# A two-block transformer kernel: the modulation's accumulation and the activations' low part, both written on VectorE

## The chip, the cores and the metric

The kernel runs on one NeuronCore of a Trainium2 chip. The metric is the device time of one execution in microseconds (us). A NeuronCore has TensorE (PE in the profile, with its weight loads shown apart as PEld), VectorE (DVE), ScalarE (ACT), GpSimd (POOL) and SyncE (SP, which issues nearly all DMAs here). Each engine works through its own queue in the order in which the program wrote it, and waits at an instruction whose inputs are not there yet.

## The reference

Two transformer blocks work on 256 tokens of width 1024, all in fp32. The first has a SwiGLU feed-forward network, two attentions with a gated merge, and a second feed-forward network. The second has two layers, one with a sliding-window attention and one with a stick-breaking attention, each with a feed-forward network behind it. Six modulation vectors for each of these two layers come from a conditioning vector `c`:

```python
cond = jax.nn.silu(c)
for i in range(DEPTH_2):
    mod = (cond @ ada_w[i] + ada_b[i])[:, None, :]
    sh1, sc1, g1, sh2, sc2, g2 = jnp.split(mod, 6, axis=-1)
    ...
    h = rmsnorm_2(x, norm2_g[i]) * (1.0 + sc2) + sh2
    x = x + g2 * swiglu_2(h, w_gate[i], w_up[i], w_down[i])
...
swiglu_2 = (jax.nn.silu(h @ w_gate) * (h @ w_up)) @ w_down
```

`ada_w` is 2 x 1024 x 6144 fp32 values, 50 MB. The hidden width of every feed-forward network is 2816, which is 22 tiles of 128.

## The kernel before

Activations are kept transposed: channels on the 128 partitions, the 256 tokens along the free axis. TensorE takes fp32r operands, so each fp32 factor is cut into a high part (rounded) and a low part (the value minus its high part), and a product of two tiles is three matmuls, high by high, high by low and low by high (`mm3`, lines 270 to 273).

Weights come as 194 blocks of 16 tiles (1 MB each) through `Stream`. SyncE loads a block into one of four `raw` buffers. Each quarter block (128 x 512) is then cast on ScalarE (`wh`, line 211) and subtracted on VectorE (`wl`, line 219). `W.step`, called from `pump` after every four tile products, writes the next quarter into the queues, two blocks ahead of the block that TensorE works on; `wh` and `wl` have three buffers.

A feed-forward network (`ffn`) is 22 units of gate and up products, 48 matmuls each, and then 8 outputs of the down product, which take 11 weight blocks. I call these the gate-up part and the down part of FFN1 to FFN4. The activation of a unit is a generator, `epilogue`, of which `follow` takes one step after every fourth tile product of later units. Its steps before were: `tg` and `tu` on VectorE from PSUM (lines 493, 494; with a shift also two one-column copies `bb`, 497 and 498); `sg` on ScalarE (500); `a` on VectorE (505, or 503 with a shift); then, in one step, the high part `ah` on ScalarE (507) and the low part `al` on GpSimd (508). The PSUM tiles of one unit are used again two units later, so `tg` and `tu` free what TensorE needs next.

The modulation runs beside the feed-forward networks (`Ada`). It is a product of one row with a matrix, made without TensorE: a step takes one 128 x 1024 tile of `ada_w`, scales it by one column of `cs` and adds it to `acc`; eight steps give one modulation vector for each partition's share, and `reduce` sums over partitions by four pairs of VectorE transposes and reductions (452, 453) and four small matmuls (460). `A.tick` is called at the last quarter of each weight block, behind that block's third and before its last `wl`, and makes as many steps as the plan is behind: 24 steps beside FFN1, 32 each beside FFN2 and FFN3, 8 beside FFN4. Tiles are loaded up to three steps ahead into three buffers (423, 424). The step before:

```python
if kc == 0:
    self.acc = self.pool.tile([128, 1024], F32, tag="acc", bufs=2, name=nm("acc"))
    nc.scalar.activation(self.acc, raw, AF.Copy, scale=self.cs[:, 0:1])
else:
    nc.scalar.activation(raw, raw, AF.Copy, scale=self.cs[:, kc:kc + 1])
    nc.gpsimd.tensor_add(self.acc, self.acc, raw)
```

Of the kernel before, what the change touches and what calls it, by code (L numbers as in the profile page):

```python
# [10 lines left out]
F32 = mybir.dt.float32  # L11
F32R = mybir.dt.float32r
I32 = mybir.dt.int32
AF = mybir.ActivationFunctionType
ALU = mybir.AluOpType
# [3 lines left out]
S = 256  # L19
# [138 lines left out]
def hybrid_two_block_kernel(ctx: ExitStack, tc: tile.TileContext, x, w, ada, vecs, rows, pos, consts,  # L158
                            masks, out):
    nc = tc.nc  # L160
# [9 lines left out]
    def nm(s):  # L170
        count[0] += 1
        return f"{s}_{count[0]}"

    def mm_ps(shape):
        return pp.tile(shape, F32, tag="mm", bufs=4, name=nm("mm"))
# [5 lines left out]
    class Stream:  # L181
# [51 lines left out]
        def next(self, *names):  # L233
            i = self.taken
            assert {n for n, _, _ in plan[i]} <= set(names), (i, plan[i][0], names)
            self.prep(self.CUT * (i + 1))
            while any(d[0] == i for d in self.due):
                self.rest(len(self.due) - 1)
            self.taken += 1
            self.quarter = -1  # L240
            self.step()
            return self.hl.pop(i)

        def step(self):

            self.quarter += 1
            if self.quarter < 4:
                at = self.CUT * (self.taken - 1 + self.ahead) + self.quarter + 1
                self.prep(min(at, self.parts + 2))
            if self.quarter == 3:  # L250
                A.tick()
# [6 lines left out]
    def pump():  # L258
        for g in list(hooks):
            try:  # L260
                next(g)
            except StopIteration:
                hooks.remove(g)
        W.step()
# [5 lines left out]
    def mm3(ps, lh, ll, rh, rl, start, stop):  # L270
        nc.tensor.matmul(ps, lhsT=lh, rhs=rh, start=start, stop=False)  # L271
        nc.tensor.matmul(ps, lhsT=lh, rhs=rl, start=False, stop=False)  # L272
        nc.tensor.matmul(ps, lhsT=ll, rhs=rh, start=False, stop=stop)  # L273
# [111 lines left out]
    class Ada:  # L385
# [42 lines left out]
        def step(self):  # L428
            i = self.i
            if i >= self.last:  # L430
                return
            self.load(i + 3)
            cg, kc = divmod(i, DC)
            raw = self.raw.pop(i)
            if kc == 0:
                self.acc = self.pool.tile([128, 1024], F32, tag="acc", bufs=2, name=nm("acc"))
                nc.scalar.activation(self.acc, raw, AF.Copy, scale=self.cs[:, 0:1])
            else:
                nc.scalar.activation(raw, raw, AF.Copy, scale=self.cs[:, kc:kc + 1])  # L439
                nc.gpsimd.tensor_add(self.acc, self.acc, raw)  # L440
            self.i += 1
            if kc == DC - 1:
                l, g = divmod(cg, 6)
                self.due = (self.ticks + 2, self.reduce(self.acc, l, g))
# [36 lines left out]
    def ffn(pool, names, norm, shift, add_scale, after, pair=False, table=None):  # L481
        gate, up, down = names
        n = S + 2 if shift else S
        ah = pool.tile([128, FC, S], F32R, name=nm("ah"))
        al = pool.tile([128, FC, S], F32R, name=nm("al"))
        early, tails = [], []

        def epilogue(c, ps):
            tg = pool.tile([128, S], F32, tag="tg", bufs=2, name=nm("tg"))
            tu = pool.tile([128, S], F32, tag="tu", bufs=2, name=nm("tu"))  # L490
            sg = pool.tile([128, S], F32, tag="sg", bufs=2, name=nm("sg"))
            a = pool.tile([128, S], F32, tag="a", bufs=2, name=nm("a"))
            nc.vector.tensor_mul(tg, ps[0][:, :S], norm.r)  # L493
            nc.vector.tensor_mul(tu, ps[1][:, :S], norm.r)  # L494
            if shift:
                bb = pool.tile([128, 2], F32, tag="bb", bufs=2, name=nm("bb"))
                nc.vector.tensor_copy(bb[:, 0:1], ps[0][:, S:S + 1])
                nc.vector.tensor_copy(bb[:, 1:2], ps[1][:, S:S + 1])  # L498
            yield
            nc.scalar.activation(sg, tg, AF.Silu, bias=bb[:, 0:1] if shift else 0.0)  # L500
            yield
            if shift:
                nc.vector.scalar_tensor_tensor(a, tu, bb[:, 1:2], sg, op0=ALU.add, op1=ALU.mult)
            else:
                nc.vector.tensor_mul(a, tu, sg)  # L505
            yield
            nc.scalar.copy(ah[:, c], a)  # L507
            nc.gpsimd.tensor_sub(al[:, c], a, ah[:, c])  # L508

        def follow():  # L510
            tails.extend(epilogue(*e) for e in early)
            early.clear()
            for g in list(tails):
                if next(g, tails) is tails:
                    tails.remove(g)

        c = 0
        while c < FC:
            paired = c == 0 and pair
            bank = at_ps if c in (0, 3) else mm_ps  # L520
            units = [(c, W.next(gate, up), [bank([128, n]), bank([128, n])])]
            if paired:
                W.ahead = 1
                units.append((1, W.next(gate, up), [mm_ps([128, n]), mm_ps([128, n])]))
            order = [(u, half, kc) for u in units for half in range(2) for kc in range(DC)]
            if c == 0:
                order.sort(key=lambda o: o[2] + 3 * o[0][0])
            for i, ((_, (wh, wl), ps), half, kc) in enumerate(order):
                t = half * DC + kc
                mm3(ps[half], wh[:, t], wl[:, t], xgh[:, kc, :n], xgl[:, kc, :n], kc == 0, kc == DC - 1)  # L530
                if i % 4 == 3:
                    pump()
                if i % 4 == 1 and (c > 2 or c == 2 and (pair or i > 8)):
                    follow()
            W.ahead = 2
            early.extend((at, ps) for at, _, ps in units)
            c += len(units)
        while early or tails:
            follow()
        if table:  # L540
            nc.scalar.preload_act_table_set(table)
        i = 0
        for d in range(DC):
            p = mm_ps([128, S])
            for kc in range(FC):
                if i % 16 == 0:
                    wh, wl = W.next(down)
                mm3(p, wh[:, i % 16], wl[:, i % 16], ah[:, kc], al[:, kc], kc == 0, kc == FC - 1)
                i += 1
                if i % 4 == 0:  # L550
                    pump()
            s = add_scale if isinstance(add_scale, float) else add_scale[:, d:d + 1]
            nc.vector.scalar_tensor_tensor(xT[:, d], p, s, xT[:, d], op0=ALU.mult, op1=ALU.add)  # L553
            after(d)
# [269 lines left out]
    with ExitStack() as mix:  # L824
# [73 lines left out]
        with tc.tile_pool(name="merge", bufs=1) as gp:  # L898
# [5 lines left out]
            for d in range(DC):  # L904
                if d % 4 == 0:
                    bh, bl = W.next("w_up_b")
                if d == 0:
                    W.ahead = 1
                    ah, al = W.next("w_up_a")
# [203 lines left out]
    with ExitStack() as mix:  # L1113
# [12 lines left out]
        def after(steps, act):  # L1126
            for _ in range(steps):
                yield
            act()
# [67 lines left out]
        name = "wqkv_b_2"  # L1197
# [69 lines left out]
```

## Time and profile before

| | us |
|---|---|
| median of 3 runs (lowest, highest) | 1222.14 (1218.98, 1222.35) |
| the profiled execution | 1221.54 |
| its span, first to last instruction | 1219.7 |
| TensorE busy | 1178.0 (97%) |
| VectorE busy | 977.0 (80%) |
| ScalarE busy | 716.4 (59%) |
| GpSimd busy | 435.9 (36%) |

The profiled execution has 1.84 us around its span and lies 0.60 us below the median. The page's chain of work that ended last runs almost wholly through TensorE's matmuls of lines 271 to 273. Busy times are unions of an engine's instructions; the "mean ns" of a group is the mean length of one instruction, and two instructions that follow each other closely overlap a little in these records, so busy time is below count times mean. The idle column of a group is the idle time of the engine just before it and what ended that.

### The profile page before, as it was taken

Reading aid. Unit: us, or ns where it says so; the run is one execution under the profiler, and the core shown is the slowest. Engines: PE = TensorE matmul, PEld = TensorE weight load, DVE = VectorE, ACT = ScalarE, POOL = GpSimd, SP = SyncE. Lnnn points to the kernel's source line nnn. Section 1 sums busy time; section 2 is a strip of 40 time slices with the busy share of each in tenths; the row PEclk is TensorE's granted clock in tenths of the full one; section 3 lists DMA queues with packets and bytes.
Section 4 is the critical chain, followed back from the end, with each engine's and each line's share of the span. In section 5 each row is a group of like instructions: output and inputs, shape, how many; then the busy total and the mean of one; then the engine's idle time right before and its main releaser. Section 6 shows DMA issues by size and latency. Waiting matters only on the chain. (4 is left out here: it accounts for less than half of the span.)

```text
span 1219.7 us, 24926 instructions
## 1 busy us (share of the span) xinstructions
PE 1178.0 (97%) x9762; PEld 1138.4 (93%) x9762; DVE 977.0 (80%) x1886; ACT 716.4 (59%) x1420; POOL 435.9 (36%) x338
## 2 busy tenths in 40 slices
PE   8999999999999999988998999989899999999998
PEld 7999999999899998988997899989898889999998
DVE  8879997565668899999878789998987786777652
ACT  5666664455465666575466777656546666665441
POOL 4556442011303275665246046655510002342100
PEclk9999999999999999999998999999999999999999
DMA  8876666434344686865451277676663334764450
GB/s 315 291 299 247 240 240 234 174 140 172 110 158 148 244 294 217 322 260 217 173 180 70 82 255 286 246 289 246 230 243 135 117 134 173 263 248 163 166 196 37
DMA packets 45332, 251.74 MB, mean 206 GB/s; under 512 B 5280, under 2 KB 8096, under 8 KB 21536
## 3 DMA queue, kind: packets, MB, share of 16 engines
q1 hardware_dynamic: 44784, 248.78, 56.2%
q8 instruction: 77, 1.26, 0.4%
q10 hardware_dynamic: 432, 1.38, 0.3%
q14 instruction: 39, 0.32, 0.1%
HBM read 249.09 MB, written 1.05 MB: 205 GB/s over the span
## 5 line engine op out<-in xcount | busy, mean ns | idle before, releaser
L219 DVE TENSOR_TENSOR wl<-raw,wh 128x512 fp32r<-128x512 f32 x744 | 624.3, 877 | 60.6 <-ACT wh L211 59.2
L271 PE MATMUL mm<-xgh,wh 128*128 128x256 f32 (+1 forms) x1840 | 526.0, 286 | 12.4 <-DVE tg L493 7.1
L273 PE MATMUL mm<-xgh,wl 128*128 128x256 f32 (+1 forms) x1840 | 520.1, 283 | 0.0
L272 PE MATMUL mm<-xgl,wh 128*128 128x256 f32 (+1 forms) x1840 | 519.0, 282 | 0.0
L211 ACT CAST wh<-raw 128x512 fp32r<-128x512 f32 (+1 forms) x752 | 419.9, 613 | 162.0 <-PE mm L272 80.4
L271 PEld LDWEIGHTS mm<-xgh,wh 128*128 128x128 f32 x1840 | 348.0, 189 | 20.9 <-issue 20.5
L272 PEld LDWEIGHTS mm<-xgl,wh 128*128 128x128 f32 x1840 | 349.2, 190 | 0.0
L273 PEld LDWEIGHTS mm<-xgh,wl 128*128 128x128 f32 x1840 | 348.1, 189 | 0.3 <-DVE wl L219 0.3
L440 POOL TENSOR_TENSOR acc<-acc,ada 128x1024 f32<-128x1024 f32 x84 | 215.1, 2561 | 186.3 <-ACT ada L439 185.6
L273 PE MATMUL mm<-ah,wl 128*128 128x256 f32 x704 | 197.8, 281 | 3.1 <-DVE wl L219 3.1
L271 PE MATMUL mm<-ah,wh 128*128 128x256 f32 x704 | 197.8, 281 | 2.5 <-DVE bb L498 2.5
L272 PE MATMUL mm<-al,wh 128*128 128x256 f32 x704 | 197.3, 280 | 0.0
L273 PEld LDWEIGHTS mm<-ah,wl 128*128 128x128 f32 x704 | 132.7, 188 | 4.0 <-DVE wl L219 3.9
L271 PEld LDWEIGHTS mm<-ah,wh 128*128 128x128 f32 x704 | 132.9, 189 | 2.8 <-issue 2.6
L272 PEld LDWEIGHTS mm<-al,wh 128*128 128x128 f32 x704 | 133.1, 189 | 0.0
L340 POOL TENSOR_TENSOR ssq<-ssq,sq 128x256 f32<-128x256 f32 x49 | 41.9, 861 | 251.9 <-ACT sq L335 250.9
L508 POOL TENSOR_TENSOR al<-a,ah 128x256 fp32r<-128x256 f32 x88 | 94.7, 1079 | 98.8 <-ACT ah L507 98.8
L439 ACT ACTIVATE ada<-ada,cs 128x1024 f32<-128x1024 f32 x84 | 95.5, 1147 | 0.0
L335 ACT ACTIVATE sq<-xT 128x256 f32<-128x256 f32 x49 | 19.7, 412 | 83.6 <-DVE xT L553 75.1
L494 DVE TENSOR_TENSOR tu<-mm,rB 128x256 f32<-128x256 f32 x80 | 33.1, 414 | 44.2 <-PE mm L273 44.2
L860 POOL TENSOR_SCALAR bias<-M 128x384 f32<-128x384 f32 x20 | 25.5, 1281 | 100.7 <-DVE lo L702 100.1
L507 ACT CAST ah<-a 128x256 fp32r<-128x256 f32 x88 | 34.8, 398 | 44.0 <-DVE a L505 29.8
(201 smaller groups left out, 1465.0 us busy)
## 6 DMA issues: line engine op xcount, KB each, us to landing
raw<-in_w SPq DMA_DIRECT2D x185, 1024.0 KB, 5.4
ada<-in_ada SPq DMA_DIRECT2D x96, 512.0 KB, 3.9
raw<-in_w SPq DMA_DIRECT2D x8, 128.0 KB, 3.9
raw<-in_w SPq DMA_DIRECT2D x4, 256.0 KB, 5.1
out<-xT SPq DMA_DIRECT2D x8, 128.0 KB, 2.1
xT<-in_x SPq DMA_DIRECT2D x3, 256.0 KB, 4.5
M<-in_masks ACTq DMA_DIRECT2D x1, 768.0 KB, 4.3
Mstick<-in_masks ACTq DMA_DIRECT2D x1, 386.0 KB, 3.3
```

The costliest lines, as they stand in the source:

```text
L211: nc.scalar.copy(h[:, part], self.raw[i][:, part])
L219: engine.tensor_sub(l[:, part], self.raw[i][:, part], h[:, part])
L271: nc.tensor.matmul(ps, lhsT=lh, rhs=rh, start=start, stop=False)
L272: nc.tensor.matmul(ps, lhsT=lh, rhs=rl, start=False, stop=False)
L273: nc.tensor.matmul(ps, lhsT=ll, rhs=rh, start=False, stop=stop)
L340: nc.gpsimd.tensor_add(self.ssq, self.ssq, t)
L439: nc.scalar.activation(raw, raw, AF.Copy, scale=self.cs[:, kc:kc + 1])
L440: nc.gpsimd.tensor_add(self.acc, self.acc, raw)
L494: nc.vector.tensor_mul(tu, ps[1][:, :S], norm.r)
L507: nc.scalar.copy(ah[:, c], a)
L508: nc.gpsimd.tensor_sub(al[:, c], a, ah[:, c])
L860: nc.gpsimd.tensor_scalar(b, M[:, at:at + 384], slope, None, op0=ALU.mult)
```

## The change

The step of the modulation leaves ScalarE and GpSimd: its first product becomes one VectorE tensor-scalar operation, and each later scaling and addition becomes one VectorE operation, `acc = raw * cs + acc`. The low part `al` moves from GpSimd to VectorE and is written one step of `follow` later than `ah`, and `a` has three buffers instead of two. The title of the change also speaks of heads in pairs; the attention code is the same in both kernels.

```diff
             if kc == 0:
                 self.acc = self.pool.tile([128, 1024], F32, tag="acc", bufs=2, name=nm("acc"))
-                nc.scalar.activation(self.acc, raw, AF.Copy, scale=self.cs[:, 0:1])
+                nc.vector.tensor_scalar(self.acc, raw, self.cs[:, 0:1], None, op0=ALU.mult)
             else:
-                nc.scalar.activation(raw, raw, AF.Copy, scale=self.cs[:, kc:kc + 1])
-                nc.gpsimd.tensor_add(self.acc, self.acc, raw)
+                nc.vector.scalar_tensor_tensor(self.acc, raw, self.cs[:, kc:kc + 1], self.acc,
+                                               op0=ALU.mult, op1=ALU.add)
...
-            a = pool.tile([128, S], F32, tag="a", bufs=2, name=nm("a"))
+            a = pool.tile([128, S], F32, tag="a", bufs=3, name=nm("a"))
...
             yield
             nc.scalar.copy(ah[:, c], a)
-            nc.gpsimd.tensor_sub(al[:, c], a, ah[:, c])
+            yield
+            nc.vector.tensor_sub(al[:, c], a, ah[:, c])
```

On VectorE, one unit of the gate-up part of FFN2 was written like this before (`raw` and `wh` are a weight block and its high part, `mm` the PSUM tiles, `rB` the norm's factor):

```order
L493 TENSOR_TENSOR tg_5881<-mm_5797,rB_4841 128x256
L494 TENSOR_TENSOR tu_5882<-mm_5798,rB_4841 128x256
L219 TENSOR_TENSOR wl_5868<-raw_5719,wh_5867 128x512 x2
L505 TENSOR_TENSOR a_5884<-tu_5882,sg_5883 128x256
L219 TENSOR_TENSOR wl_5868<-raw_5719,wh_5867 128x512 x2
```

and a unit with two modulation steps is now:

```order
L493 TENSOR_TENSOR tg_6095<-mm_6002,rB_4820 128x256
L494 TENSOR_TENSOR tu_6096<-mm_6003,rB_4820 128x256
L219 TENSOR_TENSOR wl_6081<-raw_5921,wh_6080 128x512 x2
L505 TENSOR_TENSOR a_6098<-tu_6096,sg_6097 128x256
L219 TENSOR_TENSOR wl_6081<-raw_5921,wh_6080 128x512
L439 SCALAR_TENSOR_TENSOR acc_5899<-ada_5976,cs,acc_5899 128x1024
L439 SCALAR_TENSOR_TENSOR acc_5899<-ada_6064,cs,acc_5899 128x1024
L462 TENSOR_TENSOR modT_124<-at_6158,V 128x8
L219 TENSOR_TENSOR wl_6081<-raw_5921,wh_6080 128x512
L509 TENSOR_TENSOR al_5144<-a_6098,ah_5143 128x256
```

The two accumulations stand between the third and the fourth `wl` of the unit, and `al` stands last, ahead of the next unit's `tg`.

On GpSimd, the same part of FFN2 was written like this before:

```order
L440 TENSOR_TENSOR acc_5463<-acc_5463,ada_5541 128x1024
L440 TENSOR_TENSOR acc_5463<-acc_5463,ada_5617 128x1024
L508 TENSOR_TENSOR al_5165<-a_5652,ah_5164 128x256
L440 TENSOR_TENSOR acc_5463<-acc_5463,ada_5693 128x1024
L508 TENSOR_TENSOR al_5165<-a_5732,ah_5164 128x256
```

All of these are gone from GpSimd's queue, which goes from 325 rows to 153; VectorE's goes from 1573 to 1814 and ScalarE's loses the 96 modulation rows.

## Rows read from the trace of the kernel before

**Rows 1.** The page: each engine's busy time, share of the span, instructions

```profile
PE 1178.0 (97%) x9762; PEld 1138.4 (93%) x9762; DVE 977.0 (80%) x1886; ACT 716.4 (59%) x1420; POOL 435.9 (36%) x338
```

**Rows 2.** Stretches: FFN2 and FFN3 (gate-up, down), FFN1 and FFN4 (gate-up)

```profile
core 0: us, PE busy (x) PEld busy (x) DVE busy (x) ACT busy (x) POOL busy (x), PEclk, DMA share, GB/s
409.00:541.00 132.00, 123.27 (x1027) 122.03 (x1027) 126.57 (x175) 85.41 (x152) 77.42 (x43) 0.99 0.72 264
541.00:609.00 68.00, 62.26 (x531) 60.91 (x531) 59.72 (x93) 37.03 (x69) 29.58 (x21) 1.00 0.58 212
705.00:838.00 133.00, 125.14 (x1046) 123.99 (x1045) 125.71 (x213) 87.24 (x153) 76.88 (x43) 1.00 0.71 264
838.00:904.00 66.00, 62.29 (x534) 61.92 (x533) 61.66 (x92) 37.71 (x65) 27.60 (x16) 0.97 0.62 224
20.00:142.00 122.00, 121.14 (x1024) 120.88 (x1024) 105.07 (x169) 80.57 (x148) 64.44 (x39) 1.00 0.77 289
1031.00:1151.00 120.00, 119.86 (x1004) 119.49 (x1003) 88.70 (x205) 72.35 (x139) 39.03 (x31) 1.00 0.63 223
```

**Rows 3.** Waits of PE, 409 to 609, then 705 to 904: total us, times, longest

```profile
PE mm L271 <- DVE tg L493: 7.1, 5, 2.3
...
PE mm L271 <- DVE bb L498: 7.7, 5, 2.5
PE at L460 <- DVE adas L453: 3.7, 1, 3.7
```

**Rows 4.** Timelines of DVE, POOL and PE in FFN3's gate-up: start, us, instructions

```profile
791.40 4.02 DVE L219 TENSOR_TENSOR wl<-raw,wh 128x512 fp32r<-128x512 f32 x2
795.35 0.41 DVE L493 TENSOR_TENSOR tg<-mm,rB 128x256 f32<-128x256 f32 x1
...
791.16 2.59 POOL L440 TENSOR_TENSOR acc<-acc,ada 128x1024 f32<-128x1024 f32 x1
793.71 1.17 POOL L508 TENSOR_TENSOR al<-a,ah 128x256 fp32r<-128x256 f32 x1
...
796.30 0.36 PE L271 MATMUL mm<-xgh,wh 128*128 128x258 f32 x1 [2.41 <-DVE bb L498]
```

**Rows 5.** DVE groups: FFN4 down (wl), FFN4 gate-up, FFN1 down (xgh): busy, mean ns

```profile
L219 DVE TENSOR_TENSOR wl<-raw,wh 128x512 fp32r<-128x512 f32 x38 | 24.4, 687 | 11.6 <-ACT wh L211 11.6
...
L503 DVE SCALAR_TENSOR_TENSOR a<-tu,bb,sg 128x256 f32<-128x256 f32 x21 | 9.9, 475 | 0.0
L493 DVE TENSOR_TENSOR tg<-mm,rB 128x256 f32<-128x256 f32 x19 | 7.9, 414 | 0.0
...
L376 DVE TENSOR_SCALAR xgh<-xT,V 128x256 fp32r<-128x256 f32 x7 | 2.5, 354 | 0.2
```

**Rows 6.** DVE groups: FFN2 gate-up (3), FFN3 gate-up (2), FFN1 gate-up, FFN3 down

```profile
L219 DVE TENSOR_TENSOR wl<-raw,wh 128x512 fp32r<-128x512 f32 x85 | 89.2, 1079 | 3.2 <-ACT wh L211 3.1
L505 DVE TENSOR_TENSOR a<-tu,sg 128x256 f32<-128x256 f32 x21 | 21.2, 1015 | 0.6 <-POOL al L508 0.6
L493 DVE TENSOR_TENSOR tg<-mm,rB 128x256 f32<-128x256 f32 x19 | 7.8, 411 | 0.0
...
L219 DVE TENSOR_TENSOR wl<-raw,wh 128x512 fp32r<-128x512 f32 x88 | 94.3, 1107 | 1.7 <-ACT wh L211 1.7
L503 DVE SCALAR_TENSOR_TENSOR a<-tu,bb,sg 128x256 f32<-128x256 f32 x21 | 13.0, 621 | 0.0
...
L219 DVE TENSOR_TENSOR wl<-raw,wh 128x512 fp32r<-128x512 f32 x87 | 77.5, 926 | 1.8 <-ACT wh L211 1.6
...
L219 DVE TENSOR_TENSOR wl<-raw,wh 128x512 fp32r<-128x512 f32 x45 | 43.3, 1006 | 2.9 <-ACT wh L211 2.9
```

**Rows 7.** Whole run: groups of L1173 and L507, landing of the modulation's tiles

```profile
L1173 DVE TENSOR_TENSOR_SCAN left<-z,Mstick 128x386 f32<-128x386 f32 x16 | 15.3, 954 | 0.0
L507 ACT CAST ah<-a 128x256 fp32r<-128x256 f32 x88 | 34.8, 398 | 44.0 <-DVE a L505 29.8 <-DVE a L503 13.6
...
DMA to landing us min/median/max: 3.3/3.9/7.3
```

## The prediction

> **What bounds the kernel now.** I read the page first: TensorE is busy for 97% of the span, VectorE for 80%, so over the whole run TensorE is the bound [rows 1]. Then I cut the run into stretches, because these shares are averages. The modulation runs beside the feed-forward networks, and there the picture splits. In FFN1's and FFN4's gate-up parts TensorE idles for 122.0 - 121.1 = 0.9 us and for 0.1 us. In FFN2 it idles for 132.0 - 123.3 = 8.7 us in the gate-up part and 5.7 us in the down part, in FFN3 for 7.9 and 3.7 us, 26.0 us in all; and VectorE is busy there for 126.6 of 132 and 125.7 of 133 us, against 88.7 of 120 in FFN4 [rows 2]. The list of waits says what TensorE waits for in these stretches: `tg` and `bb`, the VectorE operations that free PSUM, and the modulation's sums, with single waits of 2.3 to 3.7 us [rows 3]. So FFN2 and FFN3 are bound by VectorE in bursts, and nothing else in the run is.
>
> The timeline shows what fills VectorE. Two `wl` take 4.02 us together while GpSimd runs an `acc` addition of 2.59 us and an `al` of 1.17 us; the `tg` behind them starts at 795.35, and TensorE's next matmul comes after 2.41 us of waiting [rows 4]. Undisturbed, one `wl` takes 0.687 us [rows 5]; its mean is 1.079 us in FFN2's gate-up part and 1.107 in FFN3's. `tg`, which has one operand in PSUM, takes 0.411 us in FFN2 and 0.414 in FFN4: it is not stretched [rows 5, 6]. So it is not VectorE that is slow: an operation with both tensors in SBUF is held while GpSimd works.
>
> **The change, part by part.**
>
> What goes. The 84 `acc` additions and 88 `al` leave GpSimd, and with them nearly all that holds VectorE in these stretches. Held time, as count times (mean minus undisturbed mean): FFN2 gate-up 85 x (1.079 - 0.687) = 33.3 for `wl` and 21 x (1.015 - 0.414) = 12.6 for `a`, 45.9 us; FFN3 gate-up 88 x (1.107 - 0.687) = 37.0 and 21 x (0.621 - 0.475) = 3.1, 40.1 us; FFN1 gate-up 87 x (0.926 - 0.687) = 20.8 us; FFN3 down 45 x (1.006 - 0.687) = 14.4 us [rows 5, 6]. On ScalarE 96 scalings go; it is busy for 85 of 132 us there [rows 2], so that is worth nothing by itself.
>
> What comes. No row has the 1024-column operation. A tensor-tensor operation grows from 0.414 to 0.687 us between 256 and 512 columns, 0.273 per 256; the scalar-tensor-tensor form with 256 columns takes 0.475 [rows 5]. So 1024 columns are 0.475 + 3 x 0.273 = 1.29 us. The next operation starts about 0.07 us before the last one's end (`tg` at 795.35 against 791.40 + 4.02 = 795.42 [rows 4]), so each adds 1.22 us of busy time. Upper end: the slowest operation per column in this run, the scan, takes 0.954 us for 386 columns [rows 7], which would be 2.53 us for 1024. Lower end: half the slope, 0.475 + 3 x 0.14 = 0.89. I take 1.22, since the nearest row is the same form with the same kinds of operand. The first product of each eight is a tensor-scalar operation, 0.354 us at 256 columns [rows 5], hence at most 0.354 + 3 x 0.273 = 1.17; I take 0.9. `al` is a 256-column subtraction: 0.41, adding 0.34.
>
> A gate-up part holds about 22 accumulations, 3 first products and 21 `al`: 26.8 + 2.7 + 7.1 = 36.6 us. The balance for VectorE:
>
> - FFN2 gate-up: 126.6 - 45.9 + 36.6 = 117.3 us, where TensorE needs 123.3.
> - FFN3 gate-up: 125.7 - 40.1 + 36.6 = 122.2, where TensorE needs 125.1.
> - FFN1 gate-up (some 16 accumulations, 2 first products): 105.1 - 20.8 + 19.5 + 1.8 + 7.1 = 112.7, where TensorE needs 121.1.
> - FFN3 down (7 or 8 accumulations, one first product, two `al`): 61.7 - 14.4 + 9.8 + 0.9 + 0.7 = 58.7 of 66; FFN2 down is alike.
>
> VectorE falls below TensorE everywhere, but narrowly: 95% and 98% in the two gate-up parts. What matters besides is that the bursts get shorter. A unit of 48 matmuls lasts about 5.7 us (119.9 / 1004 = 0.119 each [rows 2]). `tg` is queued at the second of a unit's 16 tile products and must be done when the unit ends, so VectorE may lag by some 4.5 us. The largest lump it now meets is two accumulations in one unit, 2.4 us; before, the two `wl` shown took 4.02 us where undisturbed ones take 2 x 0.687.
>
> So TensorE's 26.0 us of idle time in FFN2 and FFN3 shrink. To it come the slow stretches of the clock: the granted clock is 0.99 over 132 us and 0.97 over 66 us [rows 2], 1.3 + 2.0 = 3.3 us lost, beside TensorE's longest waits. I take as left: 2 us in FFN2's gate-up part, 3 in FFN3's, 1 in each down part, by FFN1's gate-up part, where VectorE is busy for 105.1 of 122 us and TensorE idles for 0.9. Gain: 26.0 + 3.3 - 7 = 22 us. The profiled execution took 1221.5 us, 0.6 below the median, so the forecast is **1199.5 us**.
>
> The rule that bears on this: the Trainium skill, "SBUF — State Buffer", section "Who interferes with whom", says that a VectorE instruction with two SBUF inputs and a GpSimd instruction that reads SBUF exclude each other for a whole instruction. By that rule the new operations, all with two SBUF inputs, stay open to what GpSimd keeps, the norms' sums above all. The rows give this a small size: FFN4's gate-up part has GpSimd busy for 39.0 us [rows 2] and its VectorE at 88.7 of 120, so TensorE waits for 0.1 us there. By the rule alone the sum would lose up to the length of each GpSimd operation that is left; by the row, nothing.
>
> **The rivals.**
>
> *A new wait in VectorE's queue.* `al` needs `ah` from ScalarE, which needs `a` from VectorE; and an accumulation needs its tile's transfer, for which ScalarE waited before. Whatever waits there holds the next `tg`. FFN2 has 123.3 - 117.3 = 6 us to spare, FFN3 3 us, over 22 units 0.27 and 0.13 us each. Against it: between `a` and `al` stand two `wl` (1.2 us) and mostly an accumulation (1.2 us), while `ah` takes 0.40 us [rows 7]; a tile lands 3.9 us after its issue in the median, 7.3 at most [rows 7], and is asked for two steps ahead, at least one unit of 5.7 us. FFN1 has 121.1 - 112.7 = 8.4 us. Were 0.45 us (a whole `ah`) to be waited for in every unit, 9.9 us per part, 3.9 + 6.9 + 1.5 = 12 us of the gain would be lost: 1212. At 0.6 us per unit, 13.2 per part, 7.2 + 10.2 + 4.8 = 22 us, it is all gone: 1221, no change.
>
> *The 1024-column operation is dear.* By the scan's pace, 2.46 us of busy time instead of 1.22, FFN2's gate-up part asks VectorE for 117.3 + 22 x 1.24 = 144.6 us, FFN3's for 149.5, FFN1's for 112.7 + 19.8 = 132.5; with the 5 to 7 us in which VectorE cannot work there, the parts last about 150, 156 and 138 instead of 132, 133 and 122, **57 us slower: 1278**. It decides from about 1.5 us per operation, where the added 25 x 0.28 us eat the margins. Against it: the scalar-tensor-tensor rows at 256 columns are only 0.06 us above the plain ones.
>
> *VectorE is not released.* If `wl` is stretched by something other than GpSimd, the 36.6 us come on top: 163 us in FFN2's gate-up part, 162 in FFN3's, 133 in FFN1's: +31, +29 and +11 us, 1292. The Trainium skill, "VectorE: DVE Perf Modes", section "Rules for kernel authors", would have one keep the count of VectorE instructions low, and this adds 184. Against it speak the undisturbed means in FFN4 and the unstretched `tg` [rows 5, 6].
>
> **How the numbers follow.** VectorE released and TensorE's idle time mostly gone (1192 to 1209): 0.70. A partial gain, because of waits in the queue (1209 to 1218): 0.13. No change, by the same waits in full: 0.09. A dear operation: 0.06; not released: 0.02. Runs of this kernel tell 0.3%, 3.7 us, from no change. So faster 0.83, same 0.09, slower 0.08. The range goes from all 29.3 us gone, 1192, up to 1214, half-way into the partial gain.
>
> **What would show it.** Right: no GpSimd operation of 2.6 us; GpSimd's busy time down from 436 to about 126 us; `wl` at a mean near 0.70 in FFN2's and FFN3's gate-up parts; the new operation at 1.29 us; ScalarE's busy time down by 109 us; VectorE's about where it was; TensorE's idle time in the four stretches from 26 to about 7 us, its waits for `tg` and `bb` nearly gone. Wrong: `wl` still above 0.9 us; idle time on VectorE in front of `al` or of the accumulations; an accumulation above 1.5 us; waits of TensorE for `tg` as long as before.

## The result, and the profile after

The changed kernel takes 1188.83 us (median of 4 runs, 1187.56 to 1190.96) against 1221.84 us before (4 runs, 1218.98 to 1222.35): a ratio of 0.9736, 95% interval 0.9715 to 0.9757. That is 33 us faster where I forecast 22, and 3.2 us below the low end of my range. The profiled execution took 1188.8 us.

The page, in the order of [rows 1]:

```profile
span 1187.0 us, 24693 instructions
...
PE 1169.7 (99%) x9762; PEld 1132.9 (95%) x9762; DVE 964.4 (81%) x2070; ACT 620.9 (52%) x1324; POOL 129.4 (11%) x166
```

GpSimd's busy time fell by 306 us, and VectorE, which got 184 instructions more, is busy for 13 us less. The stretches, with the columns of [rows 2], each shifted to hold nearly the same work (TensorE's counts differ by up to 13 matmuls): FFN2's gate-up and down part, FFN3's, and FFN1's gate-up part.

```profile
409.70:529.70 120.00, 119.32 (x1014) 118.81 (x1014) 116.57 (x222) 59.88 (x126) 1.19 (x1) 1.00 0.76 292
529.70:592.20 62.50, 62.50 (x542) 62.19 (x542) 54.12 (x101) 30.87 (x62) 9.01 (x12) 1.00 0.64 227
685.20:808.20 123.00, 122.89 (x1033) 122.37 (x1033) 119.24 (x256) 64.86 (x130) 2.35 (x3) 1.00 0.74 283
808.20:871.20 63.00, 63.00 (x546) 62.69 (x546) 57.38 (x103) 28.68 (x56) 5.24 (x6) 1.00 0.68 254
20.70:142.70 122.00, 121.54 (x1028) 121.19 (x1027) 112.03 (x214) 62.34 (x131) 2.29 (x1) 1.00 0.78 289
```

In the four stretches of FFN2 and FFN3 TensorE idles for 0.7 + 0 + 0.1 + 0 = 0.8 us, where it idled for 26.0, and its clock is granted in full. Its only wait in the two gate-up parts is no longer one for VectorE (waits of PE, FFN2's gate-up part: total us, times, longest):

```profile
PE at L360 <- POOL rtok L370: 0.7, 1, 0.7
```

What VectorE now does, by groups, answers to [rows 6]; first FFN2's gate-up part, the last line FFN3's:

```profile
L219 DVE TENSOR_TENSOR wl<-raw,wh 128x512 fp32r<-128x512 f32 x85 | 56.6, 685 | 1.4 <-ACT wh L211 1.3
L439 DVE SCALAR_TENSOR_TENSOR acc<-ada,cs,acc 128x1024 f32<-128x1024 f32 x22 | 28.2, 1281 | 0.2
L437 DVE TENSOR_SCALAR acc<-ada,cs 128x1024 f32<-128x1024 f32 x4 | 3.0, 748 | 0.0
L509 DVE TENSOR_TENSOR al<-a,ah 128x256 fp32r<-128x256 f32 x21 | 8.7, 419 | 0.0
...
L219 DVE TENSOR_TENSOR wl<-raw,wh 128x512 fp32r<-128x512 f32 x88 | 59.0, 696 | 0.1
```

`wl` is back at about its undisturbed 0.687 us, and neither the accumulations nor `al` wait in front. A burst as the prediction feared it most, two accumulations in one unit, in the timeline of VectorE in FFN3 (start, us, instruction):

```profile
760.01 0.69 DVE L219 TENSOR_TENSOR wl<-raw,wh 128x512 fp32r<-128x512 f32 x1
760.61 2.61 DVE L439 SCALAR_TENSOR_TENSOR acc<-ada,cs,acc 128x1024 f32<-128x1024 f32 x2
...
763.81 0.42 DVE L509 TENSOR_TENSOR al<-a,ah 128x256 fp32r<-128x256 f32 x1
764.14 0.42 DVE L493 TENSOR_TENSOR tg<-mm,rB 128x256 f32<-128x256 f32 x1
```

Two accumulations take 2.61 us, `tg` follows 0.92 us after them, and TensorE notices nothing.

**Where the 33 us came from.** Cut by the same events in both traces, from the first `tg` of a network to its last `xT`: FFN2 shrank from 195.46 to 177.90 us, 17.6 less, and FFN3 from 191.93 to 178.92, 13.0 less. The attention between them went from 100.77 to 97.80, 3.0 less. The start grew by 0.7 us, what follows FFN3 (the second layer's attention and FFN4) grew by 0.1. The sum is 32.7 us.

### The profile page after: what moved, and what is told of

Read it like the earlier page. It is cut to its first block, busy times and chain, and to the rows that moved or that the text cites. A ratio compares the mean times of both kernels' runs of the same rounds, so it can differ in the third digit from the quotient of the medians.

```text
span 1187.0 us, 24693 instructions
## 1 busy us (share of the span) xinstructions
PE 1169.7 (99%) x9762; PEld 1132.9 (95%) x9762; DVE 964.4 (81%) x2070; ACT 620.9 (52%) x1324; POOL 129.4 (11%) x166
## 5 line engine op out<-in xcount | busy, mean ns | idle before, releaser
L219 DVE TENSOR_TENSOR wl<-raw,wh 128x512 fp32r<-128x512 f32 x744 | 501.1, 707 | 51.8 <-ACT wh L211 50.5
L439 DVE SCALAR_TENSOR_TENSOR acc<-ada,cs,acc 128x1024 f32<-128x1024 f32 x84 | 107.5, 1280 | 0.6
L507 ACT CAST ah<-a 128x256 fp32r<-128x256 f32 x88 | 35.4, 405 | 20.6 <-DVE a L505 13.5
L500 ACT ACTIVATE sg<-tg,bb 128x256 f32<-128x256 f32 x44 | 22.4, 508 | 32.3 <-DVE bb L498 31.8
L272 PE MATMUL at<-xgl,wh 128*128 128x256 f32 (+1 forms) x128 | 37.2, 291 | 1.6 <-DVE xgl L377 1.4
L509 DVE TENSOR_TENSOR al<-a,ah 128x256 fp32r<-128x256 f32 x88 | 36.5, 419 | 1.9 <-ACT ah L507 1.9
```

The source lines that it names most:

```text
L219: engine.tensor_sub(l[:, part], self.raw[i][:, part], h[:, part])
L439: nc.vector.scalar_tensor_tensor(self.acc, raw, self.cs[:, kc:kc + 1], self.acc, op0=ALU.mult, op1=ALU.add)
L509: nc.vector.tensor_sub(al[:, c], a, ah[:, c])
```

## The experiments

Each kernel is the changed one or the one before with one edit. "Changed" is 1188.83 us; ratios are to the kernel before, which ran again beside each group of experiments (medians 1219.54 to 1220.21 us), with 95% intervals. Single runs have no interval. The cuts leave out where `junk` buffers are allocated and cleared.

### Which part of the change brings the gain

**mod_only**: the changed kernel with `al` back on GpSimd, in the step of `ah`, and two buffers of `a`.

```diff
-            yield
-            nc.vector.tensor_sub(al[:, c], a, ah[:, c])
+            nc.gpsimd.tensor_sub(al[:, c], a, ah[:, c])
```

> The changed kernel with the low part back on GpSimd (same step as the high part, two buffers of a): the modulation's part of the change alone. Demand theory (TensorE idles in a gate-up part as far as VectorE's own work plus held time exceeds TensorE's need of 119 us in FFN2 and 123 us in FFN3): VectorE drops 7 us of al per part and is held by 21 al of 1.08 us, about 13 us, so FFN2 asks 116.6 - 7 + 13 = 123 us and FFN3 125: TensorE idles 2 to 4 us in each, 1194 us in all (1191 to 1199). Lump theory (only holds of 2.6 us and pairs of them hurt): 1189 to 1190. ScalarE theory (the gain comes from the 110 us of scalings that leave ScalarE): 1189.

Measured: 1190.17 us, 0.9758 [0.9744, 0.9773]. The modulation alone brings nearly everything; the interval overlaps the changed kernel's. FFN2's gate-up part in groups:

```profile
L439 DVE SCALAR_TENSOR_TENSOR acc<-ada,cs,acc 128x1024 f32<-128x1024 f32 x22 | 32.2, 1464 | 0.2
...
L508 POOL TENSOR_TENSOR al<-a,ah 128x256 fp32r<-128x256 f32 x21 | 28.8, 1374 | 88.8 <-ACT ah L507 88.8
```

An `al` on GpSimd still holds VectorE: the accumulations take 1.464 instead of 1.281 us, 22 x 0.18 = 4.0 us, and the 4 first products 1.009 instead of 0.748, 1.0 us. That is less than half of the 13 us I had expected. As `al` on VectorE costs 21 x 0.34 = 7 us there, its move is about a wash. The total, 1190.17 us, is what the lump theory had said (and about what the ScalarE theory had, which act_scale tests), and just below the 1191 to 1199 of the demand theory, which had sized the hold too large; the runs with extra VectorE work further down tell the two apart.

**al_only**: the kernel before with `al` on VectorE as the change has it, and `a` with three buffers.

```diff
-            nc.gpsimd.tensor_sub(al[:, c], a, ah[:, c])
+            yield
+            nc.vector.tensor_sub(al[:, c], a, ah[:, c])
```

> The kernel before with the low part on VectorE a step later and three buffers of a: the other part alone. Demand theory: in FFN2's gate-up part the held time falls from 46 to the 33 that the accumulations make, and 7 us of al come: 126.6 - 13 + 7 = 121 against 119: 6 us gained in FFN2 and 5 in FFN3, 1210 us (1204 to 1217). Lump theory: the long holds stay, 1217 to 1222. ScalarE theory: no change, 1222.

Measured: 1228.99 us, 1.0075 [1.006, 1.009]. This half of the change by itself makes the kernel **slower**, where every theory had said faster or no change. The time lies in FFN3's gate-up part, 134.9 us long from its first to its last `tg` where it had been 126.2. There, waits of VectorE and of TensorE, and the group of `al`:

```profile
DVE al L509 <- ACT ah L507: 8.8, 10, 1.5
...
PE mm L271 <- DVE bb L498: 11.3, 12, 1.6
```

```profile
L509 DVE TENSOR_TENSOR al<-a,ah 128x256 fp32r<-128x256 f32 x22 | 28.6, 1304 | 9.1 <-ACT ah L507 8.8
```

The timelines of VectorE, ScalarE and GpSimd show one such wait:

```profile
808.83 2.43 DVE L509 TENSOR_TENSOR al<-a,ah 128x256 fp32r<-128x256 f32 x1 [1.19 <-ACT ah L507]
...
806.32 1.15 ACT L437 ACTIVATE acc<-ada,cs 128x1024 f32<-128x1024 f32 x1
807.37 1.13 ACT L439 ACTIVATE ada<-ada,cs 128x1024 f32<-128x1024 f32 x1
808.41 0.39 ACT L507 CAST ah<-a 128x256 fp32r<-128x256 f32 x1
...
808.58 2.40 POOL L440 TENSOR_TENSOR acc<-acc,ada 128x1024 f32<-128x1024 f32 x1 [4.81 <-ACT ada L439]
```

`ah` stands behind two scalings on ScalarE, VectorE waits 1.19 us for it, and then `al` itself is held until the `acc` addition is over, 2.43 us instead of 0.42. So the rival of a new wait in VectorE's queue is a real mechanism in this kernel, where the accumulations are still on GpSimd. What keeps it out of the changed kernel, act_scale shows below.

**al_later**: al_only with `al` one step later still (two `yield`s, four buffers of `a`), meant to tell that wait from the hold of `al`.

```diff
-            yield
-            nc.vector.tensor_sub(al[:, c], a, ah[:, c])
+            yield
+            yield
+            nc.vector.tensor_sub(al[:, c], a, ah[:, c])
```

> The kernel before with the low part on VectorE, two steps of follow later than the high part (and four buffers of a). In the run with one step later, VectorE waited 8.8 us for ah in FFN3 and 3.9 us in FFN2, and the kernel took 9 us longer than before. Queue-wait theory (the loss is VectorE standing at al for ScalarE's ah, which comes behind the modulation's scalings): the waits are gone, FFN3's gate-up part is 7 to 9 us shorter, 1220 us (1216 to 1223). Holding theory (al on VectorE is held by the long additions, and that is the loss): it stays at 1227 to 1230.

Measured: 1217.71 us, 0.998 [0.9971, 0.999], 11 us less than al_only; FFN3's gate-up part is 126.2 us long again. VectorE does the same operations, so their number had not made al_only slow. The wait and the hold are not told apart, though: in FFN3's gate-up part the waits for `ah` shrank from 8.8 to 0.5 us, and the mean of `al` fell with them from 1.304 to 0.694 us, so in its new place it is held less (VectorE's busy time from the first to the last `tg` went from 126.0 to 118.9 us).

```profile
DVE al L510 <- ACT ah L507: 0.5, 1, 0.5
...
L510 DVE TENSOR_TENSOR al<-a,ah 128x256 fp32r<-128x256 f32 x22 | 15.2, 694 | 0.5 <-ACT ah L507 0.5
```

**al_same_step**: the changed kernel without the step between `ah` and `al`.

```diff
             nc.scalar.copy(ah[:, c], a)
-            yield
             nc.vector.tensor_sub(al[:, c], a, ah[:, c])
```

> The changed kernel with al in the same step as ah, directly behind it in the program: VectorE must wait there for ScalarE's ah, about 0.5 us (one cast may stand ahead of it). Demand theory: 22 x 0.5 = 11 us more in each gate-up part: TensorE idles 3 to 8 us in FFN2 and FFN3 each, 1199 us (1192 to 1206). If the wait is covered (VectorE behind ScalarE anyway, because it is the fuller engine): 1189.

Measured: 1188.87 us, 0.9737 [0.972, 0.9753]. The wait that I had expected is covered, VectorE waits for `ah` 1.9 us in the whole run: in the changed kernel "a step later" is worth nothing.

### GpSimd's work, or ScalarE's?

The change takes both away. act_scale and pool_add put one back as useless work, one operation per modulation step on a buffer `junk`.

**act_scale**: a scaling on ScalarE, as before the change.

```diff
+            nc.scalar.activation(self.junk, self.junk, AF.Copy, scale=self.cs[:, kc:kc + 1])
             self.i += 1
```

> The changed kernel with one ScalarE scaling of a 128 x 1024 scratch tile added to every modulation step, so that ScalarE is as loaded as before and GpSimd is not. It computes the same output. Demand and lump theories: 1189 us (to 1191), TensorE's idle time in FFN2 and FFN3 stays under 2 us. ScalarE theory: most of the gain is lost, 1210 to 1222.

Measured: 1189.5 us, 0.975 [0.9734, 0.9767]. ScalarE is busy for 84.0 us again from the first to the last `tg` of FFN2's gate-up part, and VectorE (111.0) and TensorE (113.1 of 113.1) do not feel it:

```profile
416.60:529.70 113.10, 113.10 (x963) 112.80 (x962) 111.00 (x206) 84.00 (x146) 0.00 (x0) 1.00 0.74 292
```

It also shows why the changed kernel has no new wait for `ah`. The scalings stand ahead of `ah` on ScalarE again, as in al_only, yet VectorE waits for `ah` 1.9 us in the whole run, four times, exactly as in the changed kernel. The timelines of ScalarE and VectorE in FFN3:

```profile
760.60 2.34 ACT L444 ACTIVATE junk<-junk,cs 128x1024 f32<-128x1024 f32 x2
762.84 0.39 ACT L511 CAST ah<-a 128x256 fp32r<-128x256 f32 x1
...
761.30 2.60 DVE L442 SCALAR_TENSOR_TENSOR acc<-ada,cs,acc 128x1024 f32<-128x1024 f32 x2
764.49 0.41 DVE L513 TENSOR_TENSOR al<-a,ah 128x256 fp32r<-128x256 f32 x1
```

While ScalarE scales, VectorE accumulates: `ah` is ready at 763.23, and VectorE comes to `al` at 764.49. Without the two accumulations it would have come there some 1.2 us too early, by these times.

**pool_add**: an addition on GpSimd, as before the change.

```diff
+            nc.gpsimd.tensor_add(self.junk, self.junk, self.junk)
             self.i += 1
```

> The changed kernel with one GpSimd addition on a 128 x 1024 scratch tile added to every modulation step; nothing waits for it. Demand theory: GpSimd's 77 us in FFN2's gate-up part held VectorE for 46 us, 0.58 us per us; 22 additions of 2.6 us hold it for 33 us, so it asks 150 us in FFN2's gate-up part, 149 in FFN3's, 136 in FFN1's where TensorE needs 119, 123 and 121: slower by about 75 us, 1265 (1235 to 1280), with wl at a mean above 1 us. ScalarE theory, and any in which GpSimd does not hold VectorE: 1189.

Measured: 1310.84 us in one run. The two gate-up parts, first to last `tg`:

```profile
453.10:601.00 147.90, 115.16 (x915) 112.86 (x914) 147.37 (x206) 56.74 (x118) 52.09 (x24) 0.87 0.56 217
769.00:924.50 155.50, 124.19 (x985) 122.51 (x985) 155.01 (x251) 61.11 (x122) 56.00 (x26) 0.90 0.57 218
```

VectorE is full, with the same 206 and 251 instructions as in the changed kernel: 24 additions of GpSimd make them 36 us longer in FFN2, 26 make them 39 us longer in FFN3. `wl` in FFN2's gate-up part is held again:

```profile
L219 DVE TENSOR_TENSOR wl<-raw,wh 128x512 fp32r<-128x512 f32 x81 | 74.0, 933 | 0.0
```

I had forecast that VectorE's demand would rise by some 33, 30 and 24 us in the gate-up parts of FFN2, FFN3 and FFN1 (to 150, 149 and 136 us, from the changed kernel's 116.6, 119.2 and 112.0). From first to last `tg` it rose by 36, 39 and 31 us, somewhat more. The total that I derived, 1265, was too low by 46 us: TensorE's waits grew long (one of 16.1 us), and the granted clock fell to 0.87 and 0.90 over these parts, 0.961 over the run. So held VectorE time is the mechanism, but this large overload cost more than its balance says.

**pool_set**: on GpSimd an operation that reads nothing, a memset of 2048 columns, per step.

```diff
+            nc.gpsimd.memset(self.junk, 0.0)
             self.i += 1
```

> The changed kernel with a GpSimd memset of a 128 x 2048 scratch tile in every modulation step: GpSimd is busy beside VectorE, but writes only. If holding needs a GpSimd operation that reads SBUF, wl stays at a mean under 0.70 us in FFN2's gate-up part and the time at 1189 us (1187 to 1192); if any GpSimd operation holds VectorE, wl goes up and the time with it, above 1200.

Measured: 1194.7 us in one run, between the two forecasts. Groups of FFN2's gate-up part:

```profile
L444 POOL MEMSET junk<- 128x2048 f32 x30 | 55.3, 1842 | 1.7
...
L219 DVE TENSOR_TENSOR wl<-raw,wh 128x512 fp32r<-128x512 f32 x93 | 63.0, 696 | 1.8 <-ACT wh L211 1.6
...
L440 DVE TENSOR_SCALAR acc<-ada,cs 128x1024 f32<-128x1024 f32 x4 | 4.2, 1044 | 0.0
```

GpSimd is busy for 55 us and `wl` stays at 0.696 us: it is not GpSimd's being busy that holds VectorE's two-input operations, but its reading. The Trainium skill, "SBUF — State Buffer", section "Who interferes with whom", says the same: a VectorE instruction with two SBUF inputs contends with a GpSimd instruction that reads SBUF, not with one that only writes it.

Operations with one tensor input are another matter: beside the memsets some of them are held. The first products take 1.044 us in the mean where they take 0.748 in the changed kernel, and a scaling of 16 columns that takes 0.17 us there lasts until a memset has ended (timelines of GpSimd and VectorE):

```profile
406.50 1.82 POOL L406 MEMSET junk<- 128x2048 f32 x1
...
407.04 1.31 DVE L770 TENSOR_SCALAR nsink<-R 128x16 f32<-128x16 f32 x1
```

TensorE's waits in FFN2 are 5.9 us (2.1 for `adas`, 2.0 for `wl`, 1.8 for `rtok`), against 0.7 us for `rtok` in the changed kernel. How much of the 5.9 us by which the kernel is slower comes from these holds, no run shows.

### How much room VectorE has left

**dve_half, dve_1, dve_2**: the changed kernel with useless 256-column subtractions behind each `al`: one in every second unit, one in each, two in each.

```diff
             nc.vector.tensor_sub(al[:, c], a, ah[:, c])
+            for _ in range(c % 2):
+                nc.vector.tensor_sub(junk, a, ah[:, c])
```

(`range(1)` and `range(2)` in the other two.)

> The changed kernel with one more VectorE subtraction of 128 x 256 in every other unit (44 in all, 3.7 us per gate-up part). From the first to the last tg, VectorE was busy for 111.1 of 113.1 us in FFN2's gate-up part and 116.0 of 117.6 in FFN3's, with TensorE never idle; with one subtraction in every unit 117.6 of 118.3 and 122.4 of 122.8. Demand theory (such a part lasts as long as the fuller engine needs, VectorE's work plus 0.5 to 1 us): 115.5 and 120.3 us, that is 2.4 and 2.7 us longer, 1194 us (1191 to 1196). If the lag that the PSUM buffers allow covers a small excess: 1189 to 1190.

> The changed kernel with one more VectorE subtraction of 128 x 256 into a scratch tile behind every al (88 in all, 0.34 us each). It measures how near to TensorE's need VectorE's load may come before TensorE idles. VectorE asks 116.6 + 7.5 = 124 us in FFN2's gate-up part and 126.7 in FFN3's, where TensorE needs 119.3 and 122.9; FFN1 119.5 of 121.5. Demand theory: the excess of 4.8 and 3.8 us, plus some 3 us in which VectorE cannot work, less a lag of up to 4.5 us that the PSUM buffers allow: 1 to 5 us per part, 1194 us (1190 to 1199). Lump theory: no long operation is added, 1189.

> The same with two subtractions (176, 15 us per gate-up part): VectorE asks 131.5 us in FFN2's, 134 in FFN3's, 127 in FFN1's gate-up part. Demand theory: 8 to 12 us longer in FFN2 and FFN3, 1 to 5 in FFN1: 1211 us (1205 to 1220). Lump theory: 1189 to 1192.

Measured: 1191.76 us, 0.9769 [0.9754, 0.9783]; 1198.26 us, 0.9817 [0.9802, 0.9831]; and 1219.86 us, 0.9994 [0.9985, 1.0003]. From the first to the last `tg` of the gate-up parts of FFN2 and FFN3, the changed kernel, then dve_half, dve_1 and dve_2:

```profile
416.40:529.60 113.20, 113.20 (x964) 112.90 (x963) 111.06 (x206) 57.41 (x120) 0.00 (x0) 1.00 0.75 293
692.10:809.70 117.60, 117.60 (x992) 117.28 (x991) 115.93 (x251) 61.04 (x122) 0.00 (x0) 1.00 0.76 291
```

```profile
414.90:530.00 115.10, 115.10 (x981) 114.80 (x980) 114.04 (x216) 57.69 (x120) 0.00 (x0) 1.00 0.74 287
693.20:812.80 119.60, 119.19 (x1003) 118.69 (x1003) 119.03 (x261) 61.69 (x122) 0.00 (x0) 1.00 0.75 288
```

```profile
416.70:535.00 118.30, 116.93 (x994) 116.42 (x993) 117.47 (x227) 58.00 (x120) 0.00 (x0) 1.00 0.73 280
698.30:821.10 122.80, 119.97 (x1006) 119.08 (x1005) 122.31 (x272) 61.72 (x122) 0.00 (x0) 1.00 0.74 280
```

```profile
421.20:549.10 127.90, 120.67 (x1005) 119.42 (x1004) 126.36 (x248) 57.26 (x120) 0.00 (x0) 0.99 0.69 260
712.30:844.80 132.50, 122.58 (x1011) 120.36 (x1011) 131.30 (x293) 60.92 (x122) 0.00 (x0) 1.00 0.70 262
```

Three things are to be seen. In the changed kernel VectorE is busy for 98% and 99% of these parts, and TensorE still loses nothing. In dve_half the part of FFN2 is 1.9 us longer with no idle time on TensorE: 17 more matmuls (x981 against x964, 0.117 us each, 2.0 us) lie ahead of the last `tg`, so VectorE has fallen behind, and TensorE has run ahead of it. As the lag is used up TensorE waits: in FFN2 it is 30 matmuls further in dve_1 and 41 (4.8 us) in dve_2, and idles there for 1.4 and 7.2 us; in FFN3, where the changed kernel already counts 992 matmuls before the last `tg`, it is 14 and 19 further. With two subtractions the part lasts little longer than VectorE's work: 127.9 for 126.4 us, 132.5 for 131.3. The times lie in the ranges of the demand theory; the lump theory, for which operations this short cost nothing (1189, and 1189 to 1192), is out. Two extra subtractions per unit, 60 us of VectorE time in the run, eat the whole gain.

### Repeats

> The kernel before once more, for its profile: do TensorE's half-speed stretches come at the same places, that in the sliding-window attention (6.8 us long) among them? If they follow the waits of the kernel, the granted clock is again about 0.994 and that stretch is there again, 1221 us; if its place is chance, the clock is between 0.993 and 0.998 with stretches elsewhere, 1218 to 1222.

> The changed kernel once more, for its profile. In its first profile TensorE ran at full clock all through, and the sliding-window attention between FFN2 and FFN3 took 3.0 us less than before, where the granted clock fell to half for 6.8 us there. If the change keeps the clock up there, the clock is 1.0 again and that stretch 3.0 us shorter; if that is chance, a half-speed stretch of 3.4 or 6.8 us is there (as in four variants) and the stretch is 0.6 to 2.3 us shorter only, with FFN2 still 17.6 and FFN3 13.0 us shorter.

Measured: 1221.84 and 1189.09 us, one run each. In the changed kernel's second profile FFN2, the attention behind it and FFN3 take 177.90, 97.78 and 178.92 us by the same events, within 0.02 us of the first; its granted clock is 0.998, with 3.4 us at half clock near the start of the run. The kernel before had its three stretches at half clock (1.2 GHz) at nearly the same places as in its first profile: they begin 480.5, 654.6 and 862.8 us after the start of the span, and in the second 480.8, 654.8 and 863.1. The longest, 6.8 us from 654.6, lies in the attention behind FFN2. That stretch, between FFN2 and FFN3, in four profiles: before, changed, changed again, al_same_step.

```profile
609.00:705.00 96.00, 90.79 (x707) 80.16 (x707) 76.47 (x252) 63.29 (x178) 40.12 (x71) 0.96 0.34 122
```

```profile
592.20:685.20 93.00, 87.78 (x709) 77.45 (x708) 75.72 (x252) 63.21 (x178) 41.15 (x71) 1.00 0.35 126
```

```profile
592.20:685.20 93.00, 87.79 (x709) 77.50 (x708) 75.69 (x251) 63.23 (x177) 40.88 (x70) 1.00 0.34 124
```

```profile
595.00:688.00 93.00, 88.50 (x690) 77.97 (x689) 73.52 (x248) 63.23 (x177) 40.36 (x71) 0.96 0.34 123
```

The work in it is the same, and so is TensorE's idle time, 5.2 us in the first three (96.00 - 90.79, 93.00 - 87.78). The 3.0 us between before and changed are the granted clock, 0.96 against 1.00. In al_same_step, whose median equals the changed kernel's, the clock of the profiled execution is 0.96 there, with 6.8 us at half clock, and by the same events the attention is only 0.6 us shorter than before. In mod_only, act_scale and dve_half it has 3.4 us at half clock and is 2.3 us shorter. The changed kernel's own four runs had clocks of 1.000, 0.997, 1.000 and 0.996 over the whole run. So this part of the gain, up to 3 us, goes with the clock, which differs between runs of one kernel and between kernels with the same work in this stretch; why **stays open**.

## Why the prediction was right and wrong

**Right: the mechanism and VectorE's balance.** Forecast demands of 117.3, 122.2, 112.7 and 58.7 us (FFN2, FFN3 and FFN1 gate-up, FFN3 down) were measured as 116.6, 119.2, 112.0 and 57.4. The accumulation, sized at 1.29 us from rows of 256 and 512 columns, takes 1.280; `al` 0.419 against 0.41; `wl` 0.685 and 0.696 against 0.70; GpSimd's busy time 129.4 against 126. Two terms were off without weight: the first product takes 0.748 us where I took 0.9, and ScalarE lost 95.5 us of busy time, not 109, since its records overlap (in the traces of al_only and act_scale two scalings in a row take 2.19 to 2.34 us, one 1.15). As the row of FFN4 had said, the 17.8 us of work that GpSimd keeps in the four stretches cost TensorE little: 0.7 us, for `rtok`.

**Wrong: the step "I take as left: 2 us in FFN2's gate-up part, 3 in FFN3's, 1 in each down part".** 0.8 us are left. My own balance put VectorE below TensorE's need in every part, and my own figure for the lag (4.5 us) was larger than the largest lump (2.4 us); from these two follows no idle time at all. I put in a reserve all the same, taken from FFN1, whose 0.9 us of idle time had another cause: it is one wait for a sum on GpSimd (`ssq`), none for VectorE. The dve runs show how sharp the edge is: a VectorE at 98% costs nothing, and the cost begins where its work outgrows TensorE's by about the lag.

**Wrong: the ceiling of 29.3 us, "all gone, 1192", as the low end of the range.** FFN2 and FFN3 gave 30.6 us. By the events used above, FFN2 and FFN3 before, then changed:

```profile
415.98:611.44 195.46, 181.67 (x1525) 179.28 (x1524) 183.03 (x256) 119.88 (x213) 105.81 (x62) 0.99 0.66 242
712.21:904.14 191.93, 180.49 (x1521) 179.18 (x1521) 182.25 (x297) 120.93 (x209) 102.11 (x56) 0.99 0.68 253
```

```profile
416.68:594.58 177.90, 177.90 (x1523) 177.29 (x1522) 167.37 (x309) 88.14 (x181) 9.01 (x12) 1.00 0.70 266
692.38:871.30 178.92, 178.92 (x1521) 178.29 (x1521) 171.53 (x351) 89.55 (x177) 5.24 (x6) 1.00 0.73 277
```

Between these events 25.2 us were idle time of TensorE (the other 0.8 of my 26.0 lie outside them), all of it gone, and its busy time for the same matmuls fell by 5.3 us. Each network had one stretch of 3.4 us at half clock, which costs half its length, so the two explain 3.4 of these 5.3 us (I had read 3.3 off the rounded clocks); the other 1.9 us are the term that the ceiling lacked. A likely reason for them, argued and not shown by a run, is that a matmul's modelled end covers the start of the wait behind it, so that TensorE's idle time was read a little too small. And the attention gave 3.0 us that I had not looked at: I had read the granted clock in the stretches of FFN2 and FFN3 alone. That they came in full in the profiled execution is luck as far as the forecast goes, since in mod_only, act_scale, dve_half and al_same_step less of them came. The 10.7 us between forecast and profiled execution are, to 0.1 us, the 7 of reserve, 1.3 above the ceiling, 0.3 of rounding and 3.0 of the attention, less 0.7 at the start and 0.1 behind FFN3.

**The rivals.** A new wait in VectorE's queue: in the changed kernel VectorE waited 0.5 us for `ah`, once, in FFN2's down part (four such waits in the whole run, 1.9 us):

```profile
DVE al L509 <- ACT ah L507: 0.5, 1, 0.5
```

It fell, and for the reason that I had given: the accumulations stand between `a` and `al` in VectorE's queue, and act_scale shows that they cover the wait even with the scalings ahead of `ah` on ScalarE. al_only shows the rival true of half the change, where the accumulations stay on GpSimd and cover nothing. A dear accumulation fell with 1.28 us. "VectorE is not released" fell with `wl` at 0.69 us; the Trainium skill's advice, given for chained operations, to keep the count of VectorE instructions low ("VectorE: DVE Perf Modes", "Rules for kernel authors") did not decide here: the change adds 184 of them and lowers VectorE's busy time by 12.6 us.

## What to carry to other kernels

When VectorE looks like the bound, compare each of its groups with the same group where GpSimd is idle: what two-input operations lose beside a reading GpSimd comes back when that work moves to VectorE itself, even if VectorE gets more instructions. Then set VectorE's demand against TensorE's need part by part; if it is smaller, and the largest lump is smaller than the lag that the buffers allow, forecast no idle time and add no reserve, as it came out here; and read the granted clock in the stretches between, too. A piece moved to VectorE that reads ScalarE's output should be judged by what stands ahead of that output in ScalarE's queue, and by what VectorE has to do meanwhile.

## What the runs showed of the hardware that was not expected

- Holding goes both ways. In mod_only `al` on GpSimd, 0.74 us in the median between 421 and 815 us, took up to 2.49 us beside the accumulations, while those grew from 1.28 to 1.46 us.
- GpSimd memsets of 1.84 us, 30 in one part, held no `wl` (0.696 us), but they held one-input scalings: 1.044 us instead of 0.748 for 1024 columns, up to 1.31 instead of 0.17 for 16.
- VectorE at 98% and 99% busy, in the changed kernel's two gate-up parts, left TensorE without idle time.
- A second profile of the kernel before had TensorE at half clock within 0.3 us of the same places of the span as the first (480.5, 654.6 and 862.8 us); changed kernels with the same work in the attention had 0, 3.4 or 6.8 us at half clock there.
